# A hybrid decoder layer in float32: adaLN loads dealt over 18 projection quarters, more adaLN rows summed on VectorE, the last expert pair's end rearranged

## The chip, the cores and the metric

The kernel runs on one core of one Trainium2 chip. The metric is the device time of one execution in microseconds. A profiled execution gives the trace that is read here.

## What is computed

One layer over 256 tokens of width 2048, all in float32. A vector c of width 2048 gives, through `w_ada` (2048 x 12288), six modulation vectors: shift, scale and gate of the mixer (sh1, sc1, gt1) and of the experts (sh2, sc2, gt2).

```
mod = silu(c) @ w_ada + b_ada                      # sh1 sc1 gt1 sh2 sc2 gt2
h   = rmsnorm(x) * g1 * (1 + sc1) + sh1
p   = h @ w_in                                     # 6216 columns
rec = gated linear recurrence (8 heads, chunks of 64) of p
att = top-64 sparse attention by an indexer (8 heads) of p
x   = x + gt1 * (concat(rec, att) @ w_out)
h   = rmsnorm(x) * g2 * (1 + sc2) + sh2
x   = x + gt2 * moe(h)                             # 32 experts, top 1 of 4 groups, top 2 in the group
out = rmsnorm(x) * g_final
```

## The kernel before

Everything that moves is a load of 1 MiB into a tile of a ring (`pump`, line 123): a list `loads` holds them in a fixed order, all are issued from SP's queue in that order, each as soon as a slot of the ring is free, and `drop` frees a slot when its last reader has been written down. The ring has seven slots `w0` to `w6`; later stages add `TT`, `x` and `v` slots.

The program is written as a list of **units**. A unit of the input projection is one quarter of the 2048 rows of `w_in` (kq, 512 rows) for one group g of 512 columns; it is worked in two halves, and each half (an item `i` of the main loop) is 24 matmuls of 256 columns, or 12 of 512. Products are made in three parts for precision: `cut` (line 443) copies a half to a rounded `wh` on ScalarE (line 448) and subtracts it on VectorE to give the rest `wl` (line 451); the matmuls are `wh` by hi(x), `wh` by lo(x), `wl` by hi(x) (lines 457 to 459, or 463 to 465). Cuts are made NSP = 3 halves ahead. TensorE, VectorE and ScalarE run their instructions in the order written, so the main loop sets the order of the work: after the matmuls of half i come the evacuation of a finished group, the cut of half i + 3, deferred work (`due`), the events of half i (`finish`), and a step or more of the jobs in `advance`: the indexer's scores and its top-64 (max and match-replace on VectorE), the attention, the recurrence and their outputs.

The adaLN work is fed between the halves in two forms. sc1 and sh1 are needed first, in blocks of 512 columns (`pairs`: block 1 to 3, quarter 0 to 3; a pair of loads of 1 MiB, one for each vector). In `gem` (line 358) the sc1 load of a pair is summed on VectorE (line 347, four sums of 512 columns) and the sh1 load multiplied on TensorE (line 353). When a block's four pairs are through, `fold1` (line 383) turns it to columns on TensorE (line 388) and scales a quarter of x, `X[b]`; quarter kq of every unit needs `X[kq]`. The other four vectors come as **rows**: 16 loads of [128 x 2048] a vector, 64 in all, in the order sc2, sh2, gt1, gt2. A row is either multiplied on TensorE, four products of 512 columns that share the array (line 353, tile `ev`), or summed on VectorE in two halves of 1024 columns (`add`, line 806: a product at line 812 for a vector's first row, a multiply-add at line 814 for the others, tile `acc2`). `on_dve` (line 821) decides: by the pattern `D_B` where no job is ready, `D_J` where one is, `D_C` in the output projection, `D_Z` for gt2 once its tile exists; 0 is TensorE. What VectorE has summed is brought into the vector's bank at its end by four products with ones (`vector_end`, line 781).

Order of the units before: the first quarter of all 12 groups, with one pair behind each (`PAIRS = range(12)`); the index keys, which need all of x (lines 1031 to 1033); then the quarters 1 to 3 group by group, 36 units, with 40 rows spread over them (`ROWS_B`). A group's first quarter is evacuated by ScalarE's copy, the sum of the other three is added to it by VectorE (line 1074, two adds of 512 columns). Behind these come the output projection (32 halves, 16 rows; line 940 on for its evacuation), the router, and 16 pairs of experts of 24 loads each: gate and up products side by side (lines 1231 and 1233), the down product (line 1257), and the scatter back to the tokens (line 1293 on TensorE, the add at line 1294 on VectorE).

In the last pair the final gain is loaded as one row and spread over the partitions by four one-row products (line 1370) with copies (line 1371), after the last gate and up product. Each of the four column blocks of the down product is scaled by `scaled` (line 1264, then the parts `yh` and `yl`), scattered into bank `st` (two of them), added, and squared on ScalarE (line 1302). The end takes the mean of the squares (line 1444), the inverse root (line 111 on GpSimd), eight multiplications by root and gain (line 1449) and eight stores of 256 KB (line 1450).

Of the kernel before, what the change touches and what calls it, by code (L numbers as in the profile page):

```python
# [16 lines left out]
P = 128  # L17
# [20 lines left out]
ORDER = [11, 10, 8, 9, 2, 0, 3, 1, 4, 6, 5, 7]  # L38
D_B, D_J, D_C, D_Z, J_MAX = (1,), (0,), (0,), (0,), 0
EV_LAG, EV_FIRST = 0, True  # L40
SUBS_A, SUBS_B, SUBS_C = (0,), (0,), (0,)
PAIRS = range(12)
ROWS_B = (1, 1, 1, 1, 1, 1, 1, 1, 2) * 4
ROWS_C = (1, 1, 1, 1, 1, 1, 1, 1, 1, 1, 1, 1, 1, 1, 1, 1)
# [11 lines left out]
def layer_kernel(ctx: ExitStack, tc: tile.TileContext, x, c, w_ada, b_ada, g_norm_mix, w_in, lb_logits,  # L56
# [110 lines left out]

    def w_unit(g, kq):
        unit(("w", g, kq), in_kp[:, 4 * kq:4 * kq + 4, g * 512:g * 512 + 512], kind="w", g=g, kq=kq)

# [7 lines left out]

    for i, g in enumerate(order):
        w_unit(g, 0)  # L180
        if i in PAIRS:
            pair_load()
# [9 lines left out]
    def row_event():  # L192
        event("u", *row_load())

    for i, g in enumerate(order):
        if not i:
            unit(("ikw",), in_kp[:, :, 6144:6216], kind="k")
        for kq in (1, 2, 3):
            w_unit(g, kq)
            for _ in range(ROWS_B[3 * i + kq - 1]):  # L200
                row_event()
    for part in (1, 0):
        for n in range(4):
# [783 lines left out]

    right = {}
    first_o = [i for i, u in enumerate(units) if u["kind"] == "o"][0]
    x_at = [None]  # L990
# [22 lines left out]
    for i, u in enumerate(units):  # L1013
# [28 lines left out]
        if u["kind"] == "w":  # L1042
            first, last = u["kq"] < 2 and not u["half"], u["kq"] in (0, 3) and u["half"]
            bk, k0 = "w", 4 * u["kq"] + 2 * u["half"]
# [40 lines left out]
        if EV_FIRST:  # L1085
            finish(i)
        if bk == "o" or u["kq"]:
            advance(NADV[i % len(NADV)])
# [198 lines left out]

    def scatter(n, ye, ST, ms=range(2)):
        sl = slice(512 * n, 512 * n + 512)
        for m in ms:  # L1290
            t = bank("st", 2)
            for i in range(2):
                PE.matmul(t, ST[:, m * P:m * P + P], ye[i], start=i == 0, stop=i == 1)  # L1293
            DVE.tensor_tensor(xr[:, m, sl], t, xr[:, m, sl], op=ALU.add)  # L1294
# [22 lines left out]
    prev = None  # L1317

    def scale_next(n):
        if prev:  # L1320
            prev[2][n] = scaled(prev[0][n], n, prev[1][1])
# [5 lines left out]
    for e0 in range(0, NE, 2):  # L1327
        XT, back_ = cur
        he = []

        def after0(kq):
            if not e0:
                if kq == 0:
                    gate(GT2, gs2, lambda: bank("st", 2))
                elif kq == 1:
                    overflow()
            if kq:
                piece((kq - 1) // 2, (kq - 1) % 2)
# [21 lines left out]
        if e0 + 2 < NE:  # L1360
# [5 lines left out]
            continue  # L1366
        gfb = take(("gf",))
        for n in range(4):
            t = bank("dn", 4)
            PE.matmul(t, first4[0:1], gfb[0:1, 512 * n:512 * n + 512], start=True, stop=True)  # L1370
            ACT.activation(gfb[:, 512 * n:512 * n + 512], t, AF.Copy)
        he.append(hidden(gu))
        before = None
        for n in range(5):
            ye = down_last(n, he, back_[1]) if n < 4 else None
            if before is not None:
                scatter(n - 1, before, back_[0])
                squares(n - 1)
            before = ye


    over = nc.values_load(flag, min_val=0, max_val=2 * S)
    with tc.If(over > 0):
# [56 lines left out]
        for n in range(4):  # L1440
            squares(n)


    DVE.tensor_reduce(rsf, ssf, axis=AX.X, op=ALU.add)  # L1444
    rsqrt(rsf, rsf, 1.0 / D)
    for n in range(4):
        sl = slice(512 * n, 512 * n + 512)
        for m in range(2):
            DVE.scalar_tensor_tensor(xr[:, m, sl], xr[:, m, sl], rsf[:, m:m + 1], gfb[:, sl], op0=ALU.mult, op1=ALU.mult)  # L1449
            SP.dma_start(out_rows[:, m, sl], xr[:, m, sl])  # L1450

# [26 lines left out]
```

## Time and profile before

| | us |
|---|---|
| median of 3 runs (lowest, highest) | 1577.29 (1573.65, 1577.80) |
| the profiled execution, by its own time | 1579.15 |
| its span in the trace | 1577.40 |
| TensorE busy in the span | 1512.5 |
| VectorE busy | 628.2 |
| ScalarE busy | 375.7 |
| bytes moved by DMA, mean rate | 579.15 MB, 367 GB/s |

Matmuls are pipelined and their ends are modelled, so TensorE counts as busy also where it is not at its full pace: the distance between the starts of two matmuls tells its pace. "Granted clock" is the share of TensorE's full clock that the chip granted. Idle time is set down to what ended last; idle time of an engine that nobody waits for costs nothing.

### The profile page before, as it was taken

To read this page: it belongs to the slowest core of one execution; us is meant where nothing else is said; L and a number is where in the kernel's file an instruction comes from. 1 tells how busy PE (TensorE), PEld (TensorE's weight loads), DVE (VectorE), ACT (ScalarE), POOL (GpSimd) and SP (SyncE) were. 2 spreads that over 40 slices of the span, in tenths; PEclk is the share of its full clock that TensorE was granted. 3 is DMA by queue.
4 is the path that set the end of the run, shared out by engine and by line. 5 is a ranking of instruction groups with operands and counts; after the bars stand their busy time and mean duration, and the time that the engine had idled before them with its cause. 6 is when DMAs were issued, how large, how long until landed. Compare 5 with 4: busy or idle time off the path is not lost. (4 is left out here: it accounts for less than half of the span.)

```text
span 1577.4 us, 21426 instructions
## 1 busy us (share of the span) xinstructions
PE 1512.5 (96%) x8919; PEld 883.2 (56%) x8919; DVE 628.2 (40%) x1173; ACT 375.7 (24%) x664; POOL 12.5 (1%) x23
## 2 busy tenths in 40 slices
PE   4799999999999998999999999999999999999996
PEld 2587898886776664443453554553554544544542
DVE  2576696565654353132332222332322322322224
ACT  3344334535444342111110110110110101101102
POOL 0000000000000000000000000000000000000000
PEclk9789999999999999999999999999999999999998
DMA  9999887667687679999999999999999999999994
GB/s 354 313 373 374 291 318 295 232 239 260 245 325 252 262 296 413 422 421 420 420 421 422 420 422 420 421 420 421 421 421 420 421 422 420 421 421 421 420 407 176
DMA packets 128848, 579.15 MB, mean 367 GB/s; under 512 B 17048, under 2 KB 17128, under 8 KB 72424
## 3 DMA queue, kind: packets, MB, share of 16 engines
q1 hardware_dynamic: 128746, 577.74, 92.0%
q8 instruction: 72, 1.18, 0.3%
q14 instruction: 30, 0.24, 0.0%
HBM read 575.60 MB, written 2.10 MB: 366 GB/s over the span
## 5 line engine op out<-in xcount | busy, mean ns | idle before, releaser
L1231 PE MATMUL gu<-w,XT 128*64 128x512 f32 x560 | 253.9, 597 | 0.0
L1233 PE MATMUL gu<-w,XT 128*64 128x512 f32 x536 | 242.6, 597 | 0.5 <-DMA w<-in_w_expert_up_dram 0.5
L1294 DVE TENSOR_TENSOR xr<-st,xr 128x512 f32<-128x512 f32 x128 | 86.7, 690 | 370.4 <-PE st L1293 370.4
L451 DVE TENSOR_TENSOR wl<-w,wh 128x1024 fp32r<-128x1024 f32 (+1 forms) x130 | 157.7, 1217 | 176.7 <-ACT wh L448 176.5
L448 ACT ACTIVATE wh<-w 128x1024 fp32r<-128x1024 f32 (+1 forms) x130 | 136.3, 1050 | 208.5 <-PE pj L465 109.6
L457 PE MATMUL pj<-hi,wh 128*128 128x256 f32 x480 | 143.8, 300 | 2.9 <-ACT hi L341 2.9
L458 PE MATMUL pj<-lo,wh 128*128 128x256 f32 x480 | 139.2, 290 | 0.1
L459 PE MATMUL pj<-hi,wl 128*128 128x256 f32 x480 | 139.0, 290 | 0.0
L1257 PE MATMUL dn<-w,he 128*64 128x512 f32 x536 | 137.4, 594 | 0.0
L1204 PE MATMUL dn<-G,xp 128*128 128x128 f32 x1024 | 121.9, 278 | 0.7 <-ACT gs L786 0.7
L1204 PEld LDWEIGHTS dn<-G,xp 128*128 128x128 f32 x1024 | 120.1, 195 | 4.2 <-ACT gs L786 2.2
L1264 DVE SCALAR_TENSOR_TENSOR ye<-dn,ws,gt2b 128x512 f32<-128x512 f32 x64 | 47.7, 745 | 169.2 <-PE dn L1257 169.2
L1231 PEld LDWEIGHTS gu<-w,XT 128*64 128x64 f32 x560 | 72.0, 136 | 76.4 <-issue 74.6
L353 PE MATMUL ev<-w,crep 128*32 128x512 f32 x616 | 87.7, 654 | 25.7 <-DMA w<-in_w_ada_dram 24.8
L341 ACT ACTIVATE yh<-ye 128x512 fp32r<-128x512 f32 x64 | 40.3, 629 | 275.9 <-DVE ye L1264 275.9
L1231 PE MATMUL gu<-v,XT 128*64 128x512 f32 x232 | 105.5, 597 | 0.0
L1233 PEld LDWEIGHTS gu<-w,XT 128*64 128x64 f32 x536 | 69.1, 136 | 65.0 <-issue 40.3
L1233 PE MATMUL gu<-v,XT 128*64 128x512 f32 x232 | 105.3, 597 | 0.1
L1239 ACT ACTIVATE gu<-gu 128x512 f32<-128x512 f32 x32 | 19.2, 599 | 359.6 <-PE gu L1233 359.6
L457 PEld LDWEIGHTS pj<-hi,wh 128*128 128x128 f32 x480 | 94.9, 198 | 17.2 <-issue 12.1
L458 PEld LDWEIGHTS pj<-lo,wh 128*128 128x128 f32 x480 | 95.1, 198 | 0.5 <-DVE lo L342 0.4
L459 PEld LDWEIGHTS pj<-hi,wl 128*128 128x128 f32 x480 | 95.0, 198 | 0.0
(315 smaller groups left out, 2129.0 us busy)
## 6 DMA issues: line engine op xcount, KB each, us to landing
w<-in_w_ada_dram SPq DMA_DIRECT2D x95, 1024.0 KB, 7.6
w<-in_w_expert_gate_dram SPq DMA_DIRECT2D x70, 1024.0 KB, 19.8
w<-in_w_expert_up_dram SPq DMA_DIRECT2D x67, 1024.0 KB, 19.8
w<-in_w_expert_down_dram SPq DMA_DIRECT2D x65, 1024.0 KB, 19.8
w<-in_w_in_dram SPq DMA_DIRECT2D x48, 1024.0 KB, 7.6
v<-in_w_expert_down_dram SPq DMA_DIRECT2D x32, 1024.0 KB, 19.8
v<-in_w_expert_gate_dram SPq DMA_DIRECT2D x29, 1024.0 KB, 19.8
v<-in_w_expert_up_dram SPq DMA_DIRECT2D x29, 1024.0 KB, 19.8
```

The costliest lines, as they stand in the source:

```text
L353: PE.matmul(out_[32 * quad:32 * quad + 32], crep[:, k, :], wt, start=first, stop=last, skip_group_check=True, tile_position=(0, 32 * quad))
L448: ACT.activation(wh, src, AF.Copy)
L451: (POOL if subs[i % len(subs)] else DVE).tensor_tensor(wl, src, wh, op=ALU.subtract)
L457: PE.matmul(o, wh[:, c_], hi(k), start=bool(start and j % 2 == 0), stop=False, skip_group_check=True)
L458: PE.matmul(o, wh[:, c_], lo(k), start=False, stop=False, skip_group_check=True)
L459: PE.matmul(o, wl[:, c_], hi(k), start=False, stop=bool(stop), skip_group_check=True)
L1204: PE.matmul(tv[:, r, :], xp[:, m, 4 * kq + r, :], G[:, m, :], start=m == 0, stop=m == 1)
L1231: PE.matmul(t[0:64], xk, wg[:, r, :], start=k == 0, stop=k == KD - 1, skip_group_check=True, tile_position=(0, 0))
L1233: PE.matmul(t[64:128], xk, wu[:, r, :], start=k == 0, stop=k == KD - 1, skip_group_check=True, tile_position=(0, 64))
L1257: PE.matmul(t[64 * j:64 * j + 64], he[j][:, f, :], wd[j], start=f == 0, stop=f == 3, skip_group_check=True, tile_position=(0, 64 * j))
L1264: DVE.scalar_tensor_tensor(ye, t, ws, gt2b[:, 512 * n:512 * n + 512], op0=ALU.mult, op1=ALU.mult)
L1294: DVE.tensor_tensor(xr[:, m, sl], t, xr[:, m, sl], op=ALU.add)
```

## The change

- The pairs are spread over 18 quarters instead of 12: behind the 12 first quarters follow the second quarters of the first six groups (11, 10, 8, 9, 2, 0), still ahead of the index keys. Pairs are loaded behind units 0, 2, 4, 6, 8, 10 and then 12 to 17. These six groups are evacuated after the first quarter (copy), after the second (an add), and after the fourth (an add); the other six as before. 30 units, not 36, follow the index keys, and the 40 rows are spread over them as 1, 1, 2.
- `on_dve` takes two rows of three where a job is ready (`D_J`), and every second one in the output projection (`D_C`) and of gt2 (`D_Z`). By the order of the instructions VectorE sums 29 rows where it summed 6, for four vectors instead of one.
- The end of the last pair: the gain is spread after the first chunk of the pair's first expert (`spread_final`), the scatter of the last pair takes a bank of `gu` for its second half, the first three blocks are multiplied by the gain as they are finished (`by_gain`, into two ring slots `xg`), and after the root ScalarE scales 1024 columns, VectorE 512 and 512, and four stores of 512 KB go out.

```diff
@@ constants
-D_B, D_J, D_C, D_Z, J_MAX = (1,), (0,), (0,), (0,), 0
+D_B, D_J, D_C, D_Z, J_MAX = (1,), (1, 1, 0), (1, 0), (1, 0), 0
-PAIRS = range(12)
-ROWS_B = (1, 1, 1, 1, 1, 1, 1, 1, 2) * 4
+PAIRS = (0, 2, 4, 6, 8, 10, 12, 13, 14, 15, 16, 17)
+AHEAD = 6
+ROWS_B = (1, 1, 2) * 10
@@ the list of units
-    for i, g in enumerate(order):
-        w_unit(g, 0)
+    for i, (g, kq) in enumerate([(g, 0) for g in order] + [(g, 1) for g in order[:AHEAD]]):
+        w_unit(g, kq, True, True)
         if i in PAIRS:
             pair_load()
...
-        for kq in (1, 2, 3):
-            w_unit(g, kq)
-            for _ in range(ROWS_B[3 * i + kq - 1]):
+        kqs = (2, 3) if i < AHEAD else (1, 2, 3)
+        for kq in kqs:
+            w_unit(g, kq, kq == kqs[0], kq == 3)
+            for _ in range(ROWS_B[n_b]):
                 row_event()
+            n_b += 1
@@ the main loop
-            first, last = u["kq"] < 2 and not u["half"], u["kq"] in (0, 3) and u["half"]
+            first, last = u["first"] and not u["half"], u["last"] and u["half"]
...
-        if bk == "o" or u["kq"]:
+        if i > first_k:
             advance(NADV[i % len(NADV)])
@@ the last pair
+    def spread_final():
+        gfb = take(("gf",))
+        for n in range(4):
+            t = bank("st", 2)
+            PE.matmul(t, first4[0:1], gfb[0:1, 512 * n:512 * n + 512], start=True, stop=True)
+            ACT.activation(gfb[:, 512 * n:512 * n + 512], t, AF.Copy)
+        return gfb
+    def by_gain(n):
+        for m in range(2):
+            DVE.tensor_tensor(xg[m][:, 512 * n:512 * n + 512], xr[:, m, 512 * n:512 * n + 512],
+                              gfb[:, 512 * n:512 * n + 512], op=ALU.mult)
...
+            if e0 == NE - 2 and kq == 0:
+                last.append(spread_final())
...
-        gfb = take(("gf",))
-        for n in range(4):
-            t = bank("dn", 4)
-            PE.matmul(t, first4[0:1], gfb[0:1, 512 * n:512 * n + 512], start=True, stop=True)
-            ACT.activation(gfb[:, 512 * n:512 * n + 512], t, AF.Copy)
+        gfb = last[0]
         he.append(hidden(gu))
...
         for n in range(5):
             ye = down_last(n, he, back_[1]) if n < 4 else None
             if before is not None:
-                scatter(n - 1, before, back_[0])
+                scatter(n - 1, before, back_[0], tags=("st", "gu"))
                 squares(n - 1)
+                if n in (1, 2):
+                    by_gain(n - 1)
             before = ye
+        by_gain(2)
...
-    for n in range(4):
-        sl = slice(512 * n, 512 * n + 512)
-        for m in range(2):
-            DVE.scalar_tensor_tensor(xr[:, m, sl], xr[:, m, sl], rsf[:, m:m + 1], gfb[:, sl], op0=ALU.mult, op1=ALU.mult)
-            SP.dma_start(out_rows[:, m, sl], xr[:, m, sl])
+    for m in range(2):
+        r, sl = rsf[:, m:m + 1], slice(1536, 2048)
+        ACT.activation(xg[m][:, 0:1024], xg[m][:, 0:1024], AF.Copy, scale=r)
+        DVE.scalar_tensor_tensor(xg[m][:, sl], xr[:, m, sl], r, gfb[:, sl], op0=ALU.mult, op1=ALU.mult)
+        DVE.tensor_scalar(xg[m][:, 1024:1536], xg[m][:, 1024:1536], r, None, op0=ALU.mult)
+        for h in range(2):
+            SP.dma_start(out_rows[:, m, 1024 * h:1024 * h + 1024], xg[m][:, 1024 * h:1024 * h + 1024])
```

SP's queue behind the first eight adaLN loads, up to the small-descriptor loads (`bc`), before:

```order
L136 DMA w_195<-in_w_in_dram 128x4x512
L136 DMA w_212<-in_w_ada_dram 128x4x512
L136 DMA w_218<-in_w_ada_dram 128x4x512
L136 DMA w_283<-in_w_in_dram 128x4x512
L136 DMA w_289<-in_w_ada_dram 128x4x512
L136 DMA w_295<-in_w_ada_dram 128x4x512
L136 DMA w_303<-in_w_in_dram 128x4x512
L136 DMA w_335<-in_w_ada_dram 128x4x512
L1005 DMA bc_163<-in_b_ada_dram 128x4x4 x2
```

and with the change (`w_in` is a unit, `w_ada` one load of a pair):

```order
L137 DMA w_195<-in_w_in_dram 128x4x512
L137 DMA w_212<-in_w_ada_dram 128x4x512
L137 DMA w_218<-in_w_ada_dram 128x4x512
L137 DMA w_283<-in_w_in_dram 128x4x512
L137 DMA w_289<-in_w_in_dram 128x4x512
L137 DMA w_295<-in_w_ada_dram 128x4x512
L137 DMA w_303<-in_w_ada_dram 128x4x512
L137 DMA w_335<-in_w_in_dram 128x4x512
L1012 DMA bc_163<-in_b_ada_dram 128x4x4 x2
```

The third unit moves ahead of the second pair's loads, and a fourth unit stands where the third pair's first load stood; four adaLN loads instead of five are in front of `bc`.

VectorE in the indexer's top-64 (tiles `sc`; `wl` is a cut, `acc` a row sum), before:

```order
L1074 TENSOR_TENSOR TT_134<-pj,TT_134 128x512 x2
L451 TENSOR_TENSOR wl<-w_1476,wh 128x1024
L507 MAX m_1780<-sc_1306 128x8
L508 MATCH_REPLACE sc_1306<-m_1780,sc_1306 128x256
L507 MAX m_1783<-sc_1306 128x8
L508 MATCH_REPLACE sc_1306<-m_1783,sc_1306 128x256
L451 TENSOR_TENSOR wl<-w_1476,wh 128x1024
```

and with the change, at a place of the same stage:

```order
L457 TENSOR_TENSOR wl<-w_1782,wh 128x1024
L820 SCALAR_TENSOR_TENSOR acc_110<-w_1786,cact,acc_110 128x1024 x2
L820 SCALAR_TENSOR_TENSOR acc_110<-w_1790,cact,acc_110 128x1024 x2
L510 TENSOR_TENSOR sc_1678<-sc_1678,cm 128x128
L513 MAX m_2056<-sc_1678 128x8
L514 MATCH_REPLACE sc_1678<-m_2056,sc_1678 128x256
L513 MAX m_2059<-sc_1678 128x8
L514 MATCH_REPLACE sc_1678<-m_2059,sc_1678 128x256
L457 TENSOR_TENSOR wl<-w_1852,wh 128x1024
```

Where a cut was followed by the indexer's work alone, two rows' sums now stand between it and the next cut.

VectorE in the last column block of the down product, up to the branch on overflow, before (`ye` and `yl` are the scaled block and its rest, `xr` the residual):

```order
L1264 SCALAR_TENSOR_TENSOR ye<-dn,ws,gt2b 128x512
L342 TENSOR_TENSOR yl<-ye,yh 128x512
L1294 TENSOR_TENSOR xr<-st,xr 128x512 x2
L1264 SCALAR_TENSOR_TENSOR ye<-dn,ws,gt2b 128x512
L342 TENSOR_TENSOR yl<-ye,yh 128x512
L1294 TENSOR_TENSOR xr<-st,xr 128x512 x4
```

and with the change (`w_10118` and `TT_10119` are the two halves of `xg`, `w_9761` the gain):

```order
L1301 TENSOR_TENSOR xr<-st,xr 128x512
L1301 TENSOR_TENSOR xr<-gu,xr 128x512
L1337 TENSOR_TENSOR w_10118<-xr,w_9761 128x512
L1337 TENSOR_TENSOR TT_10119<-xr,w_9761 128x512
L1271 SCALAR_TENSOR_TENSOR ye<-dn,ws,gt2b 128x512
L348 TENSOR_TENSOR yl<-ye,yh 128x512
L1301 TENSOR_TENSOR xr<-st,xr 128x512
L1301 TENSOR_TENSOR xr<-gu,xr 128x512
L1301 TENSOR_TENSOR xr<-st,xr 128x512
L1301 TENSOR_TENSOR xr<-gu,xr 128x512
L1337 TENSOR_TENSOR w_10118<-xr,w_9761 128x512
L1337 TENSOR_TENSOR TT_10119<-xr,w_9761 128x512
```

The multiplications by the gain stand between the blocks' adds, and those of the third block behind the last add; behind the root VectorE has four instructions of 512 columns where it had eight (line 1449).

## Rows read from the trace of the kernel before

**Rows 1.** Busy time by stretch (busy us, instructions; granted clock, DMA share, GB/s).

```profile
40.00:75.00 35.00, 26.16 (x153) 20.64 (x153) 18.55 (x24) 10.16 (x13) 0.00 (x0) 0.71 0.91 303
75.00:156.00 81.00, 76.70 (x472) 62.70 (x472) 61.18 (x99) 33.96 (x46) 0.00 (x0) 0.89 1.04 374
...
200.00:240.00 40.00, 40.00 (x335) 36.39 (x333) 37.71 (x77) 12.73 (x12) 0.00 (x0) 1.00 0.85 325
...
590.00:846.00 256.00, 251.17 (x1319) 115.52 (x1317) 73.77 (x206) 39.66 (x82) 0.70 (x1) 0.98 1.01 420
...
1536.00:1548.00 12.00, 12.00 (x40) 5.43 (x41) 2.41 (x4) 3.37 (x6) 0.00 (x0) 0.86 1.03 378
```

**Rows 2.** Timeline of one gate and up chunk of the last pair, TensorE.

```profile
1531.77 1.07 PE L1231 MATMUL gu<-w,XT 128*64 128x512 f32 x2
...
1532.55 0.13 PEld L1233 LDWEIGHTS gu<-TT,XT 128*64 128x64 f32 x1 [0.59 <-DMA TT<-in_w_expert_up_dram]
```

**Rows 3.** Timeline of TensorE, first stage (start, us, operation, idle before).

```profile
39.64 0.58 PE L457 MATMUL pj<-hi,wh 128*128 128x256 f32 x1 [2.90 <-ACT hi L341]
...
64.18 1.94 PE L353 MATMUL ev<-w,crep 128*32 128x512 f32 x8 [6.70 <-DMA w<-in_w_ada_dram]
...
74.79 0.39 PE L457 MATMUL pj<-hi,wh 128*128 128x256 f32 x1
...
101.87 0.39 PE L457 MATMUL pj<-hi,wh 128*128 128x256 f32 x1
...
107.76 1.07 PE L353 MATMUL ev<-w,crep 128*32 128x512 f32 x8
108.76 0.39 PE L457 MATMUL pj<-hi,wh 128*128 128x256 f32 x1
...
156.08 0.28 PE L1031 MATMUL pj<-hi,wh 128*72 128x256 f32 x1
```

**Rows 4.** Who waited for whom, TensorE, 30 to 156 us (total, times, longest).

```profile
PE ev L353 <- DMA w<-in_w_ada_dram: 9.0, 3, 6.7
```

**Rows 5.** VectorE's groups by line and shape, 156 to 590 us.

```profile
L451 DVE TENSOR_TENSOR wl<-w,wh 128x1024 fp32r<-128x1024 f32 x104 | 126.9, 1224 | 151.9 <-ACT wh L448 151.8
L814 DVE SCALAR_TENSOR_TENSOR acc<-w,cact,acc 128x1024 f32<-128x1024 f32 x10 | 12.4, 1277 | 0.0
L1074 DVE TENSOR_TENSOR T<-pj,T 128x512 f32<-128x512 f32 x16 | 10.9, 690 | 1.9 <-PE pj L465 1.0 <-PE pj L459 0.7
```

**Rows 6.** Line 812, the first row of a sum.

```profile
L812 DVE TENSOR_SCALAR acc<-w,cact x2: 742/744/745, 168.6 to 169.3; 128x1024 f32<-128x1024 f32 x2
```

**Rows 7.** Page, part 5: ScalarE's copy of 1024 columns.

```profile
L448 ACT ACTIVATE wh<-w 128x1024 fp32r<-128x1024 f32 (+1 forms) x130 | 136.3, 1050 | 208.5 <-PE pj L465 109.6
```

**Rows 8.** Who waited for whom, VectorE, 156 to 600 us.

```profile
DVE wl L451 <- ACT wh L448: 151.8, 83, 8.8
```

**Rows 9.** Busy time of the instructions on the indexer's scores sc alone.

```profile
156.00:330.00 174.00, 24.67 (x78) 1.00 0.77 282
```

**Rows 10.** Timeline of the end of the program, all engines.

```profile
1537.25 3.69 PE L1370 MATMUL dn<-w,first 1*128 1x512 f32 x8
...
1541.47 1.97 PE L1257 MATMUL dn<-x,he 128*64 128x512 f32 x2
...
1556.46 3.65 PE L1257 MATMUL dn<-w,he 128*64 128x512 f32 x16
...
1563.86 1.29 DVE L1294 TENSOR_TENSOR xr<-st,xr 128x512 f32<-128x512 f32 x2 [0.29 <-PE st L1293]
...
1566.28 0.16 DVE L1444 TENSOR_REDUCE rsf<-ssf 128x2 f32<-128x8 f32 x1 [1.13 <-ACTq L1383]
...
1567.59 5.39 DVE L1449 SCALAR_TENSOR_TENSOR xr<-xr,rsf,w 128x512 f32<-128x512 f32 x8 [0.95 <-POOL rsf L111]
1568.37 5.69 SPq L1450 DMA_DIRECT2D out_dram<-xr  x8
```

**Rows 11.** DMA rate from 1500 to 1577 us in 40 slices of 1.93 us.

```profile
GB/s 417 421 430 421 421 413 417 421 426 421 417 426 405 411 402 370 376 337 382 376 379 393 393 388 339 246 183 60 0 0 0 0 0 0 13 22 243 359 380 103
```

More of the change, by code (lines that the diff above doesn't have):

```diff
@@ L166, in layer_kernel, with w_unit @@
             ada_load((v, 0, q), v, 4 * q, 4, 0, 512)
-    def w_unit(g, kq):
-        unit(("w", g, kq), in_kp[:, 4 * kq:4 * kq + 4, g * 512:g * 512 + 512], kind="w", g=g, kq=kq)
+    def w_unit(g, kq, first, last):
+        unit(("w", g, kq), in_kp[:, 4 * kq:4 * kq + 4, g * 512:g * 512 + 512], kind="w", g=g, kq=kq, first=first,
+             last=last)
     pairs = [(b_, q) for b_ in range(1, 4) for q in range(4)]
@@ L193, in row_event @@
         event("u", *row_load())
+    n_b = 0
     for i, g in enumerate(order):
@@ L988, in layer_kernel @@
     right = {}
+    first_k = [i for i, u in enumerate(units) if u["kind"] == "k"][0]
     first_o = [i for i, u in enumerate(units) if u["kind"] == "o"][0]
@@ L1286, in down_last, with scatter @@
         return scaled(t, n, ws)
-    def scatter(n, ye, ST, ms=range(2)):
+    def scatter(n, ye, ST, ms=range(2), tags=("st", "st")):
         sl = slice(512 * n, 512 * n + 512)
         for m in ms:
-            t = bank("st", 2)
+            t = bank(tags[m], 2)
             for i in range(2):
@@ L1328, in layer_kernel @@
         XT, back_ = cur
-        he = []
+        he, last = [], []
         def after0(kq):
@@ L1366, in layer_kernel @@
             continue
-        gfb = take(("gf",))
-        for n in range(4):
-            t = bank("dn", 4)
-            PE.matmul(t, first4[0:1], gfb[0:1, 512 * n:512 * n + 512], start=True, stop=True)
-            ACT.activation(gfb[:, 512 * n:512 * n + 512], t, AF.Copy)
+        gfb = last[0]
         he.append(hidden(gu))
+        xg = []
+        for j in range(2):
+            pool, tag = free.pop(0)
+            xg.append(pool.tile([P, D], F32, name=tag, tag=tag))
         before = None
@@ L1441, in layer_kernel @@
             squares(n)
+        for n in range(3):
+            by_gain(n)
     DVE.tensor_reduce(rsf, ssf, axis=AX.X, op=ALU.add)
     rsqrt(rsf, rsf, 1.0 / D)
-    for n in range(4):
-        sl = slice(512 * n, 512 * n + 512)
-        for m in range(2):
-            DVE.scalar_tensor_tensor(xr[:, m, sl], xr[:, m, sl], rsf[:, m:m + 1], gfb[:, sl], op0=ALU.mult, op1=ALU.mult)
-            SP.dma_start(out_rows[:, m, sl], xr[:, m, sl])
+    for m in range(2):
[5 more added lines that the diff above has]
+            SP.dma_start(out_rows[:, m, 1024 * h:1024 * h + 1024], xg[m][:, 1024 * h:1024 * h + 1024])
 _INS = ['x', 'c', 'w_ada', 'b_ada', 'g_norm_mix', 'w_in', 'lb_logits', 'g_rec_out', 'g_att_out', 'w_out',
```

## The prediction

> **What bounds the kernel now.** I read it from the end backwards. In the experts (line 1231 on) the DMA engines are full at 420 GB/s while TensorE also counts as busy nearly all the time [rows 1]. The timeline of a late chunk settles which of the two sets the pace: the gate product of the last pair starts at 1531.77 and its partner, the up product, only at 1532.55, released by the landing of its weights [rows 2]. So late in the experts TensorE eats weights as they land. A pair needs 24 loads of 1 MiB, 25.2 MB, and at 421 GB/s that is 59.8 us. This stage therefore ends a fixed time after its stream of loads has begun, and what a change makes the earlier stages shorter comes out at the end undiminished, as long as they end on TensorE or VectorE and not on bytes. In the dense stages up to there the DMA share falls below one: 0.85 between 200 and 240 us, with TensorE at 40.00 of 40 us [rows 1]. There TensorE is the bound; VectorE beside it is at 37.71 of 40 us.
>
> The first stage is mixed. From 40 to 75 us the granted clock averages 0.71 and TensorE is busy 26.16 of 35 us [rows 1]; it waits for adaLN loads three times, 9.0 us in all, once 6.70 us [rows 3, 4]. That long wait falls behind the small-descriptor loads (bc2 and wr) in SP's queue.
>
> **Prices.** Half a projection unit: from 101.87 to 107.76 run two halves with one gap, so 2.95 us a half; the adaLN product behind them takes from 107.76 to 108.76, so 1.00 us a row of four products [rows 3]. On VectorE a row is two sums of 1277 ns, 2.55 us; the first row of a vector is two products of 744 ns [rows 5, 6]; the cut of one half (line 451) is 1224 ns and an evacuation add 690 ns [rows 5].
>
> **1. Rows that leave TensorE.** By the order of the instructions the row products drop from 58 rows to 35, so 23 rows x 1.00 = 23 us leave TensorE; four vectors instead of one must be merged back with four ones-products each, three more x 1.00 = 3 us. Net **20 us**, all in stretches where TensorE is the bound (17 to 22, since the switch to and from a row product, not the product itself, makes up part of the 1.00).
>
> **2. The first stage.** Before, from 39.64 to 74.79 (35.2 us) run 5 halves and 4 products, worth 5 x 2.95 + 4 = 18.7 us: 16.5 us lost. From 74.79 to 156.08 (81.3 us) run 19 halves and 8 products, worth 64 us; the other 17.3 us are three folds (matmuls, waits for VectorE, four updates of X) and low clock [rows 3]. The change puts 12 more halves (35.4 us) into this stage and has two unit loads, not one, between the early pairs: ahead of the small descriptors stand four unit loads and four adaLN loads instead of three and five. TensorE then has halves 3 to 6 to do where it stood still for 6.70 us. Bounds: if the stage is bound by bytes alone, its end moves by the 6 added loads, 6.3 MB / 374 GB/s [rows 1] = 17 us, and 35.4 - 17 = 18 us are won; if it is bound by TensorE alone, nothing is. Of the 16.5 us I take 11 as recovered (the slow first halves stay, and some 3 us of wait for the third pair) and 4 of the 17.3 (clock, not folds): **15 us**, bounds 0 and 18. The first stage then ends near 156 + 35.4 - 15 = 176 us. The 12 added evacuation adds (8.3 us) lie on VectorE, which is busy 61.18 of 81 us there [rows 1]: no cost, at most 2 us.
>
> **3. What VectorE gives back.** The 23 rows bring it 40 more sums x 1.277 + 6 more products x 0.744 = 55.5 us. Cover by totals is ample: before its cuts alone VectorE idles 151.8 us between 156 and 600 us, waiting for ScalarE's copy of a half whose buffers TensorE frees [rows 8]. By places it isn't. In the 12 halves from the last quarter of group 11 to the third of group 9 the new order has 12 cuts (14.7 us), 12 half-row sums (15.3), 6 evacuation adds (4.1) and about 18 of the 24.7 us that the indexer's work on its scores takes [rows 5, 9]: 52 us, against 12 x 2.95 + some 6 of products and indexer matmuls = 41 on TensorE. Of the 11 us too much VectorE's lead absorbs a part: cuts run up to three halves (8.8 us) ahead, less the copy before each of 1.05 us [rows 7] and the time to refill; I take 6 and lose 5. In the recurrence's halves, where TensorE and VectorE hand work to and fro each half, the same count gives 65 against 59 us, and in the last two groups 52 against 49; with little lead to spare I lose 4 and 3. Together **-12 us**; bounds -4 (the lead absorbs all but one place) and -22 (no lead anywhere). Waits of the output projection for VectorE's sums: -1.
>
> At the tightest place a rule bears on this. The row: VectorE at 37.71 of 40 us while TensorE loses nothing [rows 1]. The Trainium skill, page "Perfetto Trace Analysis", section "Identifying the Most-Contended Engine", holds that occupancy is a fair measure of how near VectorE is to its limit, and says to relieve the fullest engine first; by it the place has 2.3 us of room in 40, the whole 11 us are lost, and the sum would be 6 us later. The row agrees that there is no room; it doesn't show what the lead hides.
>
> **4. The end.** The gain vector's four one-row products and copies (3.69 us on TensorE from 1537.25, then line 1257 from 1541.47) move into the pair's first expert [rows 10], where each chunk has some 0.7 us of waiting to spare (from 1531.77 to 1532.55 less a product's pace) [rows 2]: -3.7 us on the path, since the loads of the last down blocks land just in time (the rate falls away only after 1546 us [rows 11]); up to 5 if the clock, 0.86 there [rows 1], stays up. Behind the last add (1563.86) the reduction waits 1.13 us for ScalarE; two gain products of 0.69 x 2 = 1.4 us now lie in that wait: +0.3; the freed bank brings -0.3. After the root, 1567.59, eight multiplications take 5.39 us and the program ends 9.8 us later [rows 10]. Now the first 512 KB store waits for one ScalarE scale, about 1.05 us [rows 7], the last for 2.2 us. But the stores are then bound by bytes: 2.1 MB at the 380 GB/s of the last full slice [rows 11] are 5.5 us: only -0.8 (0 to -2). Sum **-4.5 us**, bounds -2.5 and -7.
>
> **Sum.** -20 - 15 + 12 + 1 - 4.5 = -26.5 us. The profiled execution took 1579.15 us (span 1577.40) and would take 1552.7; it lies 1.9 us above the median of the runs, so the forecast against the median is **1551 us**. Its own range, by the bounds of terms 2 to 4 that don't fall together, is 1540 to 1562.
>
> **Rivals.**
> (a) VectorE's queue puts the sums in front of TensorE everywhere. A cut queued behind a row's sums waits for them; if the lead is eaten up early and never comes back, because the row sums hold ring slots and the cuts then also wait for late loads, all 55.5 us land on TensorE's path: -20 - 15 + 55.5 + 1 - 4.5 = +17, **1594 us**. It decides at a give-back of 38.5 us, above which the change is slower. For: the two sums of a row stand directly before the next cut, twice over at some places. Against: 151.8 us of idle time before the cuts [rows 8]. The Trainium skill, page "TensorE: Matmul & The Clock Gate", section "Architectural detail: the array is 16× 32×32, not 1× 128×128", calls the queues of VectorE and ScalarE strictly first in, first out; if that holds, no cut overtakes a sum, and no row of this trace shows one that did. Chance 0.11.
> (b) VectorE gives back 22 us or more, or the first stage wins only 5: **1567 us** (1562 to 1572.6). For: the first stage's DMA share is 1.04 already [rows 1]. 0.16.
> (c) The lead absorbs nearly everything (-4) and the first stage wins 18: **1540 us** and below. 0.12.
> (d) Losses and gains cancel but for the end: **1573 to 1582 us**. 0.06.
> (e) The forecast, 1540 to 1562: 0.55.
>
> **Chances and range.** About 0.3% (4.7 us) is what a measurement of this kernel can tell from no change. Faster: (b) + (c) + (e) = 0.83; the same 0.06; slower 0.11. The range goes from 1536 (half of (c) is left out) to 1575, leaving out (a) and half of (d): 0.06 + 0.14.
>
> **What would show it.** Right: the index-key unit (line 1031 before) begins near 176 us with 12 more halves behind it; the granted clock between 40 and 75 us is above 0.71 and no adaLN wait is near 6.70 us; the experts' first load is issued some 22 us sooner; the chunks in the late experts still wait for landings; the path from the last gate and up chunk to the down blocks has no gap of 4 us. VectorE's idle time before cuts falls by 50 us or more, and TensorE shows waits for cuts about group 9. Wrong: TensorE's waits for line 451's output of 30 us or more (then (a)), or a first stage that ends near 190 us (then (b)), or a first expert load as early as before.

## The result and the profile after

The change is slower: a median of 1591.21 us (1586.37 to 1592.61, 5 runs) against 1577.29 us (1573.65 to 1582.83, 5 runs) of the kernel before, a ratio of 1.0084 with an interval of 1.0062 to 1.0106. The forecast was 1551 us, the range 1536 to 1575; rival (a), 1594 us, came out nearest. The profiled execution took 1592.61 us with a span of 1590.7.

Busy time by stretch of the kernel after, to be read against [rows 1]:

```profile
40.00:75.00 35.00, 28.04 (x202) 24.15 (x203) 21.38 (x25) 13.18 (x16) 0.00 (x0) 0.84 0.89 295
75.00:156.00 81.00, 78.26 (x511) 66.78 (x509) 54.44 (x84) 36.40 (x46) 0.00 (x0) 0.93 0.92 326
200.00:240.00 40.00, 37.49 (x294) 33.71 (x293) 36.04 (x62) 14.19 (x18) 0.00 (x0) 0.96 0.81 305
590.00:846.00 256.00, 246.47 (x1315) 116.77 (x1317) 79.18 (x205) 43.97 (x90) 0.70 (x1) 0.98 0.97 403
846.00:1500.00 654.00, 653.08 (x3110) 318.43 (x3107) 181.89 (x401) 79.80 (x172) 0.00 (x0) 1.00 1.01 421
```

The experts run as before: 421 GB/s, and from their first load to the end of the program the span takes 986 us (before: 990), so this stage again ends a fixed time after its stream began. But that stream begins 17 us later. Its first loads, before and after:

```profile
587.28 0.33 SPq L136 DMA_DIRECT2D TT<-in_w_expert_gate_dram  x1
```

```profile
604.71 0.33 SPq L137 DMA_DIRECT2D TT<-in_w_expert_gate_dram  x1
```

So the time was lost in the dense stages. In the row for 200 to 240 us TensorE now stands still for 2.5 of 40 us and the clock, 1.00 before, is 0.96. Who waited for whom on TensorE from 200 to 610 us (total, times, longest), before:

```profile
PE mx L1168 <- DVE r L1163: 3.5, 1, 3.5
PE ev L846 <- ACT gs L786: 3.3, 2, 1.6
PE mx L958 <- DVE xp L943: 2.9, 4, 1.9
PE mx L582 <- DVE TT L576: 1.7, 1, 1.7
```

and after:

```profile
PE mx L637 <- DVE ks L691: 7.4, 2, 6.5
PE lg L977 <- DVE h2t L966: 6.4, 3, 2.5
PE mx L964 <- DVE xp L949: 6.2, 4, 1.7
PE pj L465 <- DVE wl L457: 4.7, 4, 2.5
PE ev L359 <- ACT gs L792: 2.9, 1, 2.9
PE mx L659 <- DVE tot L695: 2.5, 1, 2.5
PE mx L670 <- DVE ho L723: 2.0, 1, 2.0
```

The whole lists add up to 15.3 and 42.4 us (the router's 3.5 us, first in the list before, come behind 610 us in the change and are 3.5 there too). Only 4.7 us of the new waits are for a cut (line 457, before 451), the wait on which the prediction put nearly all of its loss. Nearly all the others are hand-overs: `ks` and `tot` of the recurrence, `h2t` and `xp` in front of the router. Here is one of them, TensorE first, then VectorE's queue in front of it:

```profile
350.79 1.08 PE L637 MATMUL mx<-qp,ks 128*32 128x32 f32 x64 [6.47 <-DVE ks L691]
```

```profile
343.11 1.23 DVE L457 TENSOR_TENSOR wl<-w,wh 128x1024 fp32r<-128x1024 f32 x1 [0.78 <-ACT wh L454]
344.25 4.87 DVE L820 SCALAR_TENSOR_TENSOR acc<-w,cact,acc 128x1024 f32<-128x1024 f32 x4
349.03 0.43 DVE L649 COPY_PREDICATED comb<-lmask,mx 128x256 f32<-128x256 int32 x1
349.36 0.69 DVE L689 TENSOR_TENSOR qp<-qp,tot 128x512 f32<-128x512 f32 x1
349.96 0.69 DVE L691 TENSOR_TENSOR ks<-ks,tot 128x512 f32<-128x512 f32 x1
```

Four half sums (two rows, line 820) hold VectorE from 344.25 to 349.03. Behind them stand the three instructions that end in the recurrence's `ks`, another 1.6 us. TensorE, whose next product in the order written needs `ks`, stands for 6.47 us.

**An account of the loss.** Every half unit's start can be read in the trace. I give each of its matmuls the pace that such matmuls have at full clock (0.118 us for 256 columns, 0.228 for 512, 1.00 for a row, for the jobs' matmuls their mean distance in the kernel before); that is the work, and what a stretch took beyond it is its loss (idle time, and time at half clock). Half unit 98 is the first of the output projection; the stretches begin where the first stage ends.

| us | first stage ends | jobs' halves, to 98: work | loss | 98 to 129: work | loss |
|---|---|---|---|---|---|
| before | 156.08 (24 halves) | 286.9 | 12.2 | 118.5 | 8.2 |
| after | 185.15 (36 halves) | 235.6 | 43.2 | 113.0 | 21.1 |

The losses behind the first stage rise from 20.4 to 64.3 us: 44 us given back. The trace gives nearly the same without any assumed pace. From the end of the first stage to half unit 129 TensorE stood still for 9.2 us before and for 40.8 us after, and it worked at half clock for 6.8 and for 29.3 us, half of which is lost: 31.7 + 11.2 = 43 us. The two stretches as wholes, with their busy TensorE (first figure behind the comma) and mean granted clock (0.99 and 0.96), before and after:

```profile
156.08:581.81 425.73, 416.58 (x3484) 325.92 (x3482) 251.28 (x362) 183.10 (x295) 9.21 (x8) 0.99 0.74 274
185.15:598.12 412.97, 372.13 (x3028) 297.01 (x3027) 286.65 (x398) 170.07 (x281) 9.21 (x8) 0.96 0.72 268
```

### The profile page after: what moved, and what is told of

Same layout as the page of the kernel before. It is cut to its first block, busy times and chain, and to the rows that moved or that the text cites. A ratio compares the mean times of both kernels' runs of the same rounds, so it can differ in the third digit from the quotient of the medians.

```text
span 1590.7 us, 21172 instructions
## 1 busy us (share of the span) xinstructions
PE 1496.7 (94%) x8759; PEld 879.3 (55%) x8759; DVE 684.6 (43%) x1233; ACT 377.8 (24%) x666; POOL 12.5 (1%) x23
## 5 line engine op out<-in xcount | busy, mean ns | idle before, releaser
L1240 PEld LDWEIGHTS gu<-w,XT 128*64 128x64 f32 x536 | 69.3, 136 | 58.3 <-issue 35.4
L469 PE MATMUL pj<-wh,hi 128*128 128x512 f32 (+1 forms) x224 | 91.1, 407 | 0.0
```

The costliest lines, as they stand in the source:

```text
L469: PE.matmul(ps, hi(k)[:, ms], wh, start=bool(start), stop=False, skip_group_check=True)
L1240: PE.matmul(t[64:128], xk, wu[:, r, :], start=k == 0, stop=k == KD - 1, skip_group_check=True, tile_position=(0, 64))
```

## The experiments

Ratios are to the kernel before, which ran beside each group (medians 1576.9 to 1577.7 us).

**1. Which part costs: rows, pairs or end.** Four kernels. The old patterns in the changed kernel:

```diff
-D_B, D_J, D_C, D_Z, J_MAX = (1,), (1, 1, 0), (1, 0), (1, 0), 0
+D_B, D_J, D_C, D_Z, J_MAX = (1,), (0,), (0,), (0,), 0
```

> The changed kernel with the three row patterns as before: pairs over 18 quarters and the new end stay, VectorE sums 3 rows instead of 29. Theory 1 (the row sums stand in VectorE's queue ahead of work that TensorE waits for): TensorE gets 26 rows back at 1.00 us, less three merges, +23 us; the 44 us that the trace of the change loses against the kernel before behind the first stage go: 1591 + 23 - 44 = 1570 us, and TensorE's waits for VectorE between 200 and 610 us fall from 42 to near the 11 us of before. Theory 2 (the pairs and the second quarters taken first are at fault): the losses stay and the rows come on top, 1605 to 1614 us; anything above 1585 speaks for it. Theory 3 (the new end costs time): 1577 to 1591.

Measured: 1569.77 us, ratio 0.9953 (0.9935 to 0.9971). The waits of TensorE between 200 and 610 us are those of before again, largest first (15.0 us in all against 15.3; the 11 us of the expectation were counted too low):

```profile
PE mx L1175 <- DVE r L1170: 3.5, 1, 3.5
PE ev L852 <- ACT gs L792: 3.3, 2, 1.6
PE mx L964 <- DVE xp L949: 2.9, 4, 1.9
```

The same edit the other way round, the new patterns in the kernel before:

> The kernel before with the three new row patterns alone (30 rows on VectorE, 24 rows fewer on TensorE). Theory 1: -24 rows x 1.00 + 3 for merges, + 44 for VectorE's queue = +23: 1600 us, and at least 1588. Theory 2: the rows leave TensorE and VectorE has room, -21 + 0 to 13: 1556 to 1569 us.

Measured: 1595.51 us, ratio 1.0119 (1.0089 to 1.0149). The end of the last pair alone, in the kernel before (the diff's hunks from "the last pair" on):

> The kernel before with the new end of the last pair alone. By term 4 of the prediction -4.5 us (-2.5 to -7): 1573 us; by the trace of the change, whose end comes some 3 us sooner behind the dense part, 1574. Theory 3 (the end costs time, because the two gain products of the scatter stand before its adds on VectorE or because four large stores start later): 1577 or more.

Measured: 1573.13 us, ratio 0.9975 (0.9953 to 0.9998): -3.7 us. And the sums shortened:

```diff
-                DVE.scalar_tensor_tensor(ah, wt, cact[:, k:k + 1], ah, op0=ALU.mult, op1=ALU.add)
+                DVE.scalar_tensor_tensor(ah[:, 0:32], wt[:, 0:32], cact[:, k:k + 1], ah[:, 0:32], op0=ALU.mult, op1=ALU.add)
```

> The changed kernel with the 50 multiply-adds of the row sums cut to 32 of their 1024 columns; the rest of these 29 rows is left out of the sums. The instructions, their order, their waits for loads and the freeing of slots stay, so the time on VectorE alone goes, some 50 x 1.2 = 60 us by the 1277 ns of one. Theory 1: the 44 us come back: 1547 us (up to 1558 if the eight first products and the twelve added evacuation adds keep a part). Theory 2, or a theory in which the sums wait for late loads and it is this wait that holds the queue: the time stays above 1580.

Measured: 1553.69 us, ratio 0.9836 (0.9805 to 0.9866), 37.5 us below the change. Theory 1 holds in all of these; theories 2 and 3 fall. The sums' time on VectorE is what costs, not the order of the loads. (Short sums also free their ring slots sooner, but TensorE's waits from 185 to 600 us, in the change, have none for a load, so the time did not go there.) Behind the first stage, TensorE's idle time falls from 40.8 to 14.4 us, and of the hand-overs `ks` falls from 7.4 to 3.2 us and `h2t` from 6.4 to 0.9; `xp` does not fall:

```profile
PE mx L964 <- DVE xp L949: 6.4, 4, 1.9
PE mx L637 <- DVE ks L691: 3.2, 2, 2.3
```

With the sums nearly free the change would be worth some 23 us; terms 1, 2 and 4 of the prediction had 39.5 for this.

**2. Where it costs, and whether by bursts.**

```diff
+D_B, D_J, D_C, D_Z, J_MAX = (1,), (1, 1, 0), (0,), (0,), 0
```

> The changed kernel with the new pattern only beside the jobs (D_J); in the output projection and for gt2 (D_C, D_Z) as before: 22 rows on VectorE, 7 back on TensorE. By the traces so far the loss behind the first stage is 64 us, of which 43 in the jobs' halves and 21 in the output projection, against 12 and 8 in the kernel before. If each place pays for its own sums: the output projection gives back 13 us of loss and takes 7 rows less a merge, +6: 1591 - 13 + 6 = 1584 us. If the output projection's loss is left over from the jobs (work that VectorE still has to catch up with), it stays: 1597 us.

Measured: 1585.05 us, ratio 1.0043 (1.0023 to 1.0062).

```diff
+D_B, D_J, D_C, D_Z, J_MAX = (1,), (0,), (1, 0), (1, 0), 0
```

> The changed kernel with the new patterns only in the output projection and for gt2 (D_C, D_Z), beside the jobs as before: 10 rows on VectorE. If each place pays for its own sums: the run with all patterns as before, 1570 us, with 7 rows less on TensorE (-6) and 13 us more loss in the output projection: 1577 us. If the output projection alone has room for its sums: 1564 us.

Measured: 1573.37 us, ratio 0.997 (0.9953 to 0.9987). Each place pays for its own sums, to within 4 us of what was expected. The third kernel spreads them:

```diff
             for h in range(2):
                 adds.append((v, k, h, ac, v not in part_acc))
-            add(2)
...
         if EV_FIRST:
             finish(i)
+        add(1 if len(adds) < 4 else 2)
```

> The changed kernel with the same 29 rows on VectorE, but a row's two half sums not one behind the other: one half sum (1.28 us) behind each half unit, two only when four are pending. Theory 1a (bursts: two or four sums in a row, 2.6 or 5.1 us, are longer than the hand-over can bear): the loss of 64 us falls to 40 or less, 1567 us or less. Theory 1b (any sum between TensorE and VectorE's steps lengthens the hand-overs, and the sums' total counts): within 8 us of 1591, 1583 to 1595.

Measured: 1578.48 us, ratio 1.0006 (0.999 to 1.0023). The fourth puts the rows behind the jobs' step (`EV_FIRST` False):

> The changed kernel with the rows of a half written behind the jobs' step of that half, not ahead of it (30 rows on VectorE, the row products on TensorE also move behind the jobs' matmuls). Theory 1a: the jobs' step no longer waits for the sums of its own half, only the next cut does, which has up to three halves of lead: 1570 us or less. Theory 1b: the sums now delay the step behind, 1583 to 1595.

Measured: 1585.41 us, ratio 1.0039 (1.002 to 1.0058). The kernel with spread sums lies between the two theories' ranges, the one with the other order in the range of 1b; neither theory is right by itself. Spreading gives 12.7 of the 44 us back, the other order 5.8. Bursts count, but sums that come in ones and twos, as all do in the kernel with spread sums, still cost most of the loss. The largest waits of the kernel with spread sums, from 185 to 600 us:

```profile
PE mx L963 <- DVE xp L948: 6.4, 4, 1.9
PE mx L637 <- DVE ks L691: 5.0, 2, 4.1
PE pj L465 <- DVE wl L457: 4.4, 3, 2.4
```

**3. Sums only where TensorE loses nothing.** Compared half unit by half unit, the change and the first kernel of experiment 1 (old patterns) show where the sums paid (us; the old patterns have more rows on TensorE in each stretch).

| half units | old patterns | change | what runs there |
|---|---|---|---|
| 52 to 58 | 23.57 | 28.25 | attention begins, cuts late behind the indexer's top-64 |
| 70 to 76 | 25.79 | 35.04 | recurrence, first head |
| 76 to 98 | 96.88 | 91.34 | end of the first head, second head (from 83), outputs |
| 98 to 114 | 61.93 | 58.14 | output projection, first part |
| 114 to 126 | 51.99 | 61.73 | second part, gt2's rows, the router's transposes |

```diff
-D_B, D_J, D_C, D_Z, J_MAX = (1,), (1, 1, 0), (1, 0), (1, 0), 0
+D_B, D_J, D_C, D_Z, J_MAX = (1,), (1, 1, 0), (1, 0), (0,), 0
+J_FROM = 76
...
-        pat = D_C if ev_at[0] >= first_o - NSP else D_J if len([j for j in jobs if set(j[2]) <= ended]) > J_MAX else D_B
+        pat = D_C if ev_at[0] >= first_o - NSP else (D_J if ev_at[0] >= J_FROM else (0,)) if len([j for j in jobs if set(j[2]) <= ended]) > J_MAX else D_B
```

> The changed kernel with rows on VectorE only where the traces so far show TensorE losing nothing by them: beside the jobs from half unit 76 on (behind the recurrence's second head), and in the first part of the output projection; none between halves 38 and 76 beyond the old pattern, none for gt2 (13 rows on VectorE). Between the run with old patterns and the change, halves 76 to 88 took 54.64 and 51.94 us, 88 to 98 42.24 and 39.40, 98 to 106 30.60 and 28.25, 106 to 114 31.33 and 29.89; sum of the differences -9.3. If each place pays for its own sums: 1570 - 9 = 1561 us. If those places were only free because VectorE's work had been done late before them, or the gain is taken by a wait for the vector's sum at the end: 1570 or more.

(Half unit 76 lies in the recurrence's first head, behind its wait for `ks`, and not behind the second head, as these words have it.)

Measured: 1562.57 us, ratio 0.9896 (0.9872 to 0.992). It beats both kernels, and by the traces' stretches: 76 to 98 took 91.84 us, 98 to 114 58.16, 114 to 126 51.91.

**4. The first stage.** The long wait of [rows 4] is still there in the change, and SP's queue shows why:

```profile
PE ev L359 <- DMA w<-in_w_ada_dram: 7.2, 3, 6.2
```

```profile
43.55 0.37 SPq L137 DMA_DIRECT2D w<-in_w_in_dram  x1
43.97 4.17 SPq L1012 DMA_DIRECT2D bc<-in_b_ada_dram  x2
48.18 2.59 SPq L1012 DMA_DIRECT2D bc<-in_g_norm_ffn_dram  x1
...
59.63 0.25 SPq L1018 DMA_DIRECT2D brow<-in_b_router_expert_dram  x1
59.98 0.39 SPq L137 DMA_DIRECT2D w<-in_w_in_dram  x1
```

From 43.97 to 59.98 us SP issues small-descriptor loads (nine more stand between these rows), and in these 16.0 us no load of 1 MiB. Two kernels move them: one to half unit 40, one to GpSimd's queue at the same place.

```diff
         if i == 8:
             masks()
+        if i == 40:
+            small_loads()
...
```

> The changed kernel with the small-descriptor loads (bc2, wr, brow) issued at half unit 40 and not ahead of the loop. In the trace of the change SP issues them from 43.97 to 59.98 us and no load of 1 MiB in between; TensorE then waits 6.19 us at 70.66 for an adaLN load. Theory 2a (SP's queue, held by them, makes that wait): it goes, and with it some of the 6.8 to 10.2 us at half clock that follow: -6 to -11, 1580 to 1585 us. Theory 2b (the first stage is bound by the bytes of its loads): the wait only shifts, 1589 to 1593. If at half 40 the queue stalls in the same way, TensorE waits there instead and nothing is won either; the first stage's end, 185 us, tells the two apart.

Measured: 1582.04 us, ratio 1.0026 (1.0005 to 1.0046), 9.2 us below the change; the first stage ends at 172.27 us, 12.9 sooner. Of these, 9.0 us lie in half units 4 to 12, where the wait was, and 4.6 in 24 to 36, whose instructions are the same but ran 3.4 and not 13.7 us at the lower clock; whether the edit did this too is not shown.

> The changed kernel with the same small-descriptor loads at the same place, issued from GpSimd's queue and not SP's. Theory 2a in its narrow form (it is SP's issuing that is held): the 1 MiB loads go on from 44 us, the wait of 6.19 us goes, 1580 to 1585 us. If it is the transfers of these small descriptors that hold the DMA engines, the 1 MiB loads are slow beside them whoever issues: 1588 to 1594.

Measured: 1589.85 us, ratio 1.0069 (1.0043 to 1.0095): against the change no difference that these runs can tell. Busy time by stretch, of the change, of the late loads, and of those on GpSimd's queue:

```profile
45.00:60.00 15.00, 14.23 (x120) 13.09 (x117) 12.34 (x15) 7.08 (x9) 0.00 (x0) 1.00 0.74 210
60.00:75.00 15.00, 8.81 (x57) 6.95 (x56) 6.29 (x7) 3.20 (x4) 0.00 (x0) 0.72 0.99 350
```

```profile
45.00:60.00 15.00, 15.00 (x123) 13.05 (x123) 12.45 (x14) 7.18 (x10) 0.00 (x0) 0.99 1.05 386
60.00:75.00 15.00, 15.00 (x127) 14.03 (x126) 10.28 (x23) 7.52 (x11) 0.00 (x0) 1.00 1.05 387
```

```profile
45.00:60.00 15.00, 14.85 (x110) 12.82 (x110) 12.10 (x16) 6.96 (x9) 0.00 (x0) 0.89 1.05 387
60.00:75.00 15.00, 15.00 (x127) 14.03 (x126) 9.90 (x12) 8.37 (x11) 0.00 (x0) 1.00 1.05 386
```

By its time the last kernel falls into the range that the transfers' theory gave; the stretches tell what happened. Theory 2a holds: with the small loads out of the way the rate from 45 to 60 us is 386 GB/s and not 210, TensorE is busy all of 45 to 75 us, and no adaLN wait is left. On GpSimd's queue the same rate is reached and the wait goes too, but the stage ends at 180.81. The first projection matmul starts at 44.50 us instead of 39.27 (40.01 with the late loads), and half units 24 to 36 take 53.07 us instead of 48.44, again with 13.7 us at the lower clock, as in the change. The hold of SP's queue makes the wait, as the narrow form says; what its end gave was lost at these two places. GpSimd's queue issued the small loads from 18.26 to 28.80 us, beside SP's first loads of 1 MiB; that they delayed the first adaLN loads is my reading of the late start, and no run separates it. The late loads were not tried in the kernel before, so how much of their gain needs the change is not known either.

**5. Both together.**

> The two edits that won, together: rows on VectorE by place (1562.6 us alone) and the small-descriptor loads at half unit 40 (9 us alone). If they add up: 1553 us, and the first stage ends near 172 us. If the small-descriptor loads at half 40 now hold up loads that TensorE needs, since it no longer waits for VectorE there: 1558 to 1566 us, with waits for DMA or cuts between 190 and 245 us.

Measured: 1552.06 us (1550.55 to 1557.50), ratio 0.9854 (0.9827 to 0.9881): they add up. The first stage ends at 171.08 us. Its TensorE waits between 200 and 610 us, and VectorE's load beside the change's from 325 to 459 us (the change first):

```profile
PE mx L1179 <- DVE r L1174: 3.5, 1, 3.5
PE mx L965 <- DVE xp L950: 2.9, 4, 1.9
PE mx L671 <- DVE ho L724: 2.0, 1, 2.0
PE ev L853 <- ACT gs L793: 1.4, 2, 0.7
```

```profile
325.00:459.00 134.00, 119.27 (x1460) 94.20 (x1459) 100.93 (x142) 53.94 (x90) 5.56 (x5) 0.96 0.70 262
```

```profile
325.00:459.00 134.00, 130.32 (x1282) 98.74 (x1269) 100.75 (x142) 61.87 (x99) 4.98 (x5) 1.00 0.81 304
```

The last kernel is some 35 us further on in its program there, so the work is not the same; but VectorE is as busy as in the change, 100.75 against 100.93 of 134 us, and TensorE, 130.32 against 119.27 us, loses little. A VectorE this full does not cost by itself; what costs is TensorE's waiting for what stands behind the sums.

## Why the prediction was wrong

**What bounds the kernel.** Right. Gains and losses of the dense stages came out at the end nearly undiminished (first expert load +17.4 us, span +13.3; about 3.0 of the 4.1 between is the new end), and the late experts still ran at 421 GB/s.

**Term 1, rows that leave TensorE (-20).** Right in size: the trace has 23 rows fewer on TensorE, and the work of all half units fell by 19 to 23 us, depending on the pace given to the jobs' matmuls (bounds 17 and 22).

**Term 2, first stage (-15).** Mis-sized. With 12 halves of 2.95 us added, the stage would end at 156.08 + 35.4 = 191.5 us; it ended at 185.15, not at 176: 6.3 us won in these two traces. The stage varies by itself: the profiles of three kernels with the old first stage end it at 151.36 to 156.08 us (mean 153.1), those of eight with the new one at 181.43 to 185.15 (mean 183.9), so 4.6 us on average. By the medians, the kernel with pairs and end is 3.4 us faster than the one with the end alone, though it has three rows more on TensorE (3 us), so about 6; the change is 4.3 us faster than the new patterns alone, of which the end's 3.7 and one row more on TensorE leave 1.6. So 2 to 6 us were won, not 15. The failed step was "TensorE then has halves 3 to 6 to do where it stood still for 6.70 us". I counted loads in SP's queue and did not time the queue. It is held for 16.0 us; the four halves are 11.8 us of work; the wait shrank only to 6.2. The granted clock between 40 and 75 us did rise, from 0.71 to 0.84. Experiment 4 shows that what I wanted was there: without the hold the stage ends at 172.27 us, and at 171.08 in experiment 5, 17 us won against the mean of before, or 14 by the medians (4.6 and 9.2). But that took an edit which the change does not have.

A rule for this case stands in the Trainium skill, "Perfetto Trace Analysis", section "What "DMA-bound" means": a kernel can be bound by the issuing engine's own queue, when that queue is solid with transfers' issue, and there large pieces are what matters. The trace agrees for the 16.0 us on SP's queue; larger pieces were tried in no run.

**Term 3, VectorE's give-back (+12, bounds 4 and 22; +1 for the output projection).** Wrong, and this turned the sign. It was 44 us by the traces (31 in the jobs' halves, 13 in the output projection), 37.5 by the run with short sums. The failed step is the model: I compared VectorE's and TensorE's totals by stretch and allowed the cuts' lead of up to three halves to absorb what was too much. That lead exists and did its work: waits for cuts were 4.7 us. In the 12 halves for which I took 5 us (half units 40 to 51) the change took 46.67 us and the old patterns 46.16 with four rows more on TensorE (4 us), so 4.5 us were lost: this part was right. But the six halves behind them, 52 to 58, for which I had no term, lost 6.7 us more (28.25 against 23.57, with two rows more); whether this is work left over from the 12 halves or their own sums is not shown. And a job's step has no lead. In the recurrence TensorE's product needs `ks` at once, and what stands in front of `ks` is paid for: a burst of four sums, 4.87 us, in a wait of 6.47. I had written that TensorE and VectorE "hand work to and fro each half" there, and took 4 us "with little lead to spare"; half units 70 to 76 alone lost 12.8. The second head and the outputs, half units 83 to 98, lost little (3.7 us of idle time): the head's steps had no sums in front of them up to 87, and never four. For the output projection, where I took 1, half units 114 to 126 took 9.7 us longer than with the old patterns (6.8 in the second kernel of experiment 2, which has the same sums there); the kernel with new patterns there and none for gt2 (experiment 3) has 51.91 us for them, so it is gt2's rows, of whose four three lie there.

**The price of a wait is more than the wait.** Of the 44 us some 32 are standing time (40.8 against 9.2 us in these halves). The rest goes with the clock: 29.3 against 6.8 us of TensorE's work ran at its lower level (1.2 GHz). Half units 70 to 76, for example, had 9.2 us of idle time, and after the waits the clock was at the lower level for 10.2 us, 5.9 of them with TensorE at work; in the old pattern 0.0 and 0.0.

**Term 4, the end (-4.5, bounds -2.5 and -7).** Right: -3.7 alone (interval -7.4 to -0.3). From the last half unit to the reduction (line 1472, before 1444) the trace shows 981.8 against 984.5 us; behind the root only 0.3 us were won (9.79 us before [rows 10], 9.49 after), where I had 0.8:

```profile
1581.25 1.15 ACT L1476 ACTIVATE w<-w,rsf 128x1024 f32<-128x1024 f32 x1 [1.80 <-POOL rsf L112]
1581.25 0.75 DVE L1477 SCALAR_TENSOR_TENSOR w<-xr,rsf,w 128x512 f32<-128x512 f32 x1 [0.95 <-POOL rsf L112]
...
1582.31 1.13 ACT L1476 ACTIVATE TT<-TT,rsf 128x1024 f32<-128x1024 f32 x1
1582.32 0.74 DVE L1477 SCALAR_TENSOR_TENSOR TT<-xr,rsf,w 128x512 f32<-128x512 f32 x1
1582.43 0.84 SPq L1480 DMA_DIRECT2D out_dram<-w  x2
...
1583.72 1.61 SPq L1480 DMA_DIRECT2D out_dram<-TT  x2
```

**The sum.** With what was measured the terms are -20, -4.6, +44 (the output projection included) and -3.7, or +15.7 us; the medians differ by +13.9.

**The rivals.** (a) gave nearly the right time, and only in part by the right way. Its mechanism, the queue of VectorE putting sums in front of TensorE, is what happened; its price (all 55.5 us) was 11 us too high, and its condition (the cuts' lead eaten up) came about for 4.7 us of waits only. That its time came out so near is partly luck: its first stage was 9 to 13 us too good, which made up for the price. Against it I held 151.8 us of VectorE's idle time before cuts [rows 8]. That was the wrong evidence: this idle time fell to 110.1 us only, and it lies at the cuts and not in front of the hand-overs.

```profile
DVE wl L457 <- ACT wh L454: 110.1, 57, 8.0
```

The rule I weighed, that an engine's occupancy is a fair measure of how near it is to its limit (the Trainium skill, "Perfetto Trace Analysis", section "Identifying the Most-Contended Engine"), would have made the loss 6 us larger, 11 us in the 12 halves it was applied to. There the runs show 4.5; only with the six halves behind them is it 11.2, so the direction was the better one for the stretch, and not for the place. And the last experiment shows a stretch as full as the change's at little loss, and the recurrence's 6.47 us came where VectorE idled soon after (3.09 us before its cut at 358.09); there occupancy did not decide. The other rule cited, that VectorE's queue is strictly first in, first out (the Trainium skill, "TensorE: Matmul & The Clock Gate", section "Architectural detail: the array is 16× 32×32, not 1× 128×128"), agrees with the four sums of 4.87 us in front of `ks`.

**What would have told it beforehand.** The order of the instructions: it has four half sums directly ahead of the recurrence's `ks`, and TensorE's next product needs `ks`. I used the order to count totals by stretch and did not follow one hand-over through both queues.

**Still open.** Why spreading the sums returned only 12.7 us was not taken apart step by step; between the two traces, half units 98 to 129 are 8.1 us shorter and the jobs' halves 5.3. Why the waits for `xp` stay when the sums are short is open too. The first stage's few us are known no better than said above: the kernel before reached half unit 24 at 156.08 us, and the same instructions up to there at 151.99 and 151.36 in the profiles of the second and third kernel of experiment 1.

## What to carry to other kernels

Idle time of an engine is room only where nobody waits for what it does next. Before moving work into an in-order queue, list the instructions behind the place it goes to and ask of each who waits for it and with how much lead: here a prefetch with three steps of lead took bursts of 5 us with 4.7 us of waits in all, while a hand-over inside a chain paid for most of one. Sort the places by that and move the work only to those that are free: with 13 of the 29 rows, and the small loads moved, the changed kernel became 1.5% faster than before, where with all 29 it was 0.8% slower.

## What was not expected

A standstill cost more than its own length: half units 4 to 12 of the change lost 10.5 us, 7.6 of them idle and the other 3 in granted clock (10.2 us at the lower level, 6.1 of them with TensorE at work); with the wait gone (late small loads) they lost 1.5 us, none of it at the lower level. And thirteen small loads of many small pieces, issued in 0.25 to 2.6 us each, kept a whole queue of 1 MiB loads back for 16.0 us, and the rate at 210 GB/s where it can be 386.
